# The opening of a transformer layer: token squares ahead of the transposes, modulation sums moved, first loads ahead

## The chip, the core and the metric

The kernel runs on one core of a Trainium2 chip. The metric is device time in microseconds (us). Its engines are named as in the profile: PE (TensorE, matmuls and transposes), PEld (its weight loads), DVE (VectorE), ACT (ScalarE), POOL (GpSimd) and SP (SyncE, whose queue issues nearly all loads).

## The reference

One layer of a hybrid backbone on 256 latent tokens with 256 context tokens ahead, width 2048, all in fp32. What matters here is its beginning:

```python
mod_x = jnp.split((jax.nn.silu(c) @ w_mod[l] + b_mod[l])[:, None, :], 6, axis=-1)
mod_c = jnp.split((jax.nn.silu(c_ctx) @ w_mod[l] + b_mod[l])[None, None, :], 6, axis=-1)
h   = rms_norm(x,   g_mix[l]) * (1 + mod_x[1]) + mod_x[0]
h_c = rms_norm(ctx, g_mix[l]) * (1 + mod_c[1]) + mod_c[0]
qa, ka, va, qb, kb, vb, rb, lrf, lrb, gate_a, gate_b = jnp.split(h @ w_in, offs, axis=-1)
```

The rest (windowed attention, gated linear attention, merge, output projection, ConvFFN) is the same in both kernels.

## The kernel before

**The tiling.** The 2048 input channels are 16 row blocks (kt) of 128. Every product with a weight is done in pieces: a weight tile `raw` of two row blocks by 512 columns (512 KB) is loaded, `wsplit` makes from it a rounded high part `whi` on ACT and the rest `wlo` on DVE (L61, L62), and PE adds three products (high by high, high by low, low by high) into a bank `acc` (L74). `proj_T` and `proj_nat` do this with the weight or the token side held in PE.

**The opening.** `x` and `ctx` come as four tiles of 128 tokens (1 MB each). Of each, the sum of squares is taken (the first half on ACT, L431, the second on DVE, L429), 16 transposes turn it (`ptx`, L436), and ACT and DVE copy the result to `xr` in turns. From the sums `token_rows` makes the row `rrow` of the factors 1/rms: a diagonal `dg` on DVE, two products `pr` on PE (L406), a copy on ACT.

**The modulation.** Shift and scale are SiLU(c) by columns of `w_mod`. The work is cut in five groups of row blocks, `groups = [(0, 2), (2, 2), (4, 4), (8, 4), (12, 4)]`. For each group and for shift and scale apart, `mod_both` makes a list of steps. A step loads a chunk `mraw` (1 MB) and adds its products into a bank `pm` (L302). The last step of a list also folds the sum: DVE transposes it to `mtr` (L305), PE adds the parts (`pcol`, L307), DVE makes four copies and adds the bias (L310, L313). Groups 0 and 1 have two steps in a list (chunks 256 columns wide), groups 2 to 4 have four (512 columns wide), so four steps a group and then eight.

**A group.** `affine_group` multiplies each row block of `xr` by scale and row factor on DVE (`xr`, L457), adds the shift on ACT, which gives the high part (`h00hi` for latent, `h10hi` for context, L458), and makes the low part on DVE (L459). Then the group's two row blocks (or four) go through the columns of QB (latent alone, two halves `j`), KB and VB (latent and context) of `w_in`. In group 0 ACT copies the sums out (`qb`, `kb`, `vb`, L474), later DVE adds to them (L476).

**What sets the order.** The code is written in the order of the work, and a scheduler places the instructions engine by engine; each engine then runs its list in order. `in_order` ties two instructions together without a wait. The steps of the next group's sums stand in `bg_steps`; `tick`, called ahead of each weight tile, takes from them at the rate `bg_rate`, so group 1's sums are spread over group 0's products, group 2's over group 1's, and so on. What is left is done ahead of the next group. Loads of the opening are chained in the order in which the code asks for them (`load`), on one queue. Each waits for the eighth load before it and for a free buffer: seven of `raw`, and sixteen 1 MB buffers (`M`) for all of `x`, `ctx`, `xr`, the `h` parts, `kb`, `vb`, the square's waste `junk` and the chunks `mraw`.

Of the kernel before, what the change touches and what calls it, by code (L numbers as in the profile page):

```python
# [8 lines left out]
F32 = mybir.dt.float32  # L9
# [7 lines left out]
P = 128  # L17
# [13 lines left out]
def layer_kernel(ctx, tc, A, out):  # L31
# [18 lines left out]
    def M(name, shape, dt=F32):  # L50
        return big.tile(shape, dt, name=name, tag="M")
# [20 lines left out]
    def mm(*a, **k):  # L72

        r = PE.matmul(*a, **k)  # L74
        last[0] = r.ins
        return r
# [8 lines left out]
    def mm_b(*a, **k):  # L85
        return after(PE.matmul(*a, **k))  # L86
# [100 lines left out]
    hold, last_lo = [], [None]  # L187

    def wsplit(src):
# [48 lines left out]
    def proj_T(w, c0, kts, rhs, evac):  # L238

        n = len(rhs)  # L240
        per = 2 // n
        banks = [acc.tile([P, 512], F32, name="acc", tag="acc") for _ in range(4 // per)]
        for k0 in kts[::2]:
            tick()
            nk = min(2, kts[-1] + 1 - k0)
            hi, lo = wsplit(w[k0 * P:(k0 + nk) * P, c0:c0 + 512])
            for part in range(2):
                for f in range(4):
                    for k in range(nk):
                        kt = k0 + k  # L250
                        w_ = (lo if part else hi)[:, k, f * P:(f + 1) * P]
                        for i, r in enumerate(rhs):
                            b = (f % per) if n == 1 else i
                            o = banks[f // per][:, b * T:(b + 1) * T]
                            ahi, alo = r(kt)
                            mm(o, w_, ahi, start=(kt == kts[0] and b == 0 and part == 0),
                                      stop=(kt == kts[-1] and part == 1), skip_group_check=True)
# [5 lines left out]
    behind = []  # L263

    def proj_pair(w, c0, kts, pair, banks, evac):

# [17 lines left out]

    ALL = list(range(KT))


    def mod_both(part, t0, n, dst):

        a = []  # L290
        c0, w = part * D + t0 * P, n * P
        nk = 16 // n

        def step(k0):
            if k0 == 0:
                a.append(bank(f"pm{part}_{t0}", (P, w), side=True))
            raw = M("mraw", [P, nk, w])
            load(raw, w_mod[k0 * P:(k0 + nk) * P, c0:c0 + w].rearrange("(c p) d -> p c d", p=P))
            for k in range(nk):
                kt = k0 + k  # L300
                q = 32 * (kt % 4)
                PE.matmul(a[0][q:q + 32, :], cS[:, kt, :], raw[:, k, :], start=(kt < 4), stop=(kt >= 12))  # L302
            if k0 == KT - nk:
                tr = W2("fb", "mtr", [P, n, 4, 32])
                V.transpose(tr.rearrange("p a b c -> p (a b c)"), a[0])  # L305
                pc = bank(f"pcol{part}_{t0}", (32, n * 4, 2))
                PE.matmul(pc, sel[:, 0:32], tr.rearrange("p a b c -> p (a b) c")[:, :, 0:2], start=True, stop=True)  # L307
                pv = pc.rearrange("p (a b) c -> p b c a", b=4)
                for b4 in range(4):
                    V.tensor_copy(dst[32 * b4:32 * b4 + 32, :, t0:t0 + n], pv[:, b4, :, :])  # L310
                b0 = part * 16 + t0
                d = dst[:, :, t0:t0 + n]
                V.tensor_tensor(d, d, bmod[:, b0:b0 + n].unsqueeze(1).to_broadcast([P, 2, n]), op=ALU.add)  # L313

        return [lambda k0=k0: step(k0) for k0 in range(0, KT, nk)]

    def mod_latent(parts, put=lambda fn: defer(3, fn), begin=None):

# [81 lines left out]
    def token_rows(tag, name, cols, mms=None):  # L400

        pr = bank("pr", (P, T), side=True)
        for t in range(2):
            dg = sm.tile([P, P], F32, name="dg", tag="t128", bufs=2)
            V.tensor_scalar(dg, ident, cols[:, t:t + 1], None, op0=ALU.mult)
            i = PE.matmul(pr[:, t * P:(t + 1) * P], ones[:, 0:P], dg, start=True, stop=True).ins  # L406
            if mms is not None:
                mms.append(i)
# [6 lines left out]
    mods = [mod_both(0, t0, n, shift1) + mod_both(1, t0, n, scale1) for t0, n in groups]  # L415

    xr = [M(f"xr{i}", [P, 8, T]) for i in range(4)]
    rrow1 = []
    junk = M("junk", [P, D])

    def load_tokens(s):
        ss = sm.tile([P, 2], F32, name="ss0", tag="ss0", bufs=2)
        for t in range(2):
            x_ = x00
            if s or t:
                x_ = M(f"x{s}{t}", [P, D])
                load(x_, A["ctx" if s else "x"][0][t * P:(t + 1) * P, :])
            if t:
                V.scalar_tensor_tensor(junk, x_, 1.0, x_, op0=ALU.mult, op1=ALU.mult, accum_out=ss[:, t:t + 1])  # L429
            else:  # L430
                S.activation(junk, x_, AF.Square, accum_out=ss[:, t:t + 1])  # L431
            for g in range(4):
                pt = bank("ptx", (P, 4, P), side=True)
                for k in range(4):
                    kt = g * 4 + k
                    PE.transpose(pt[:, k, :], x_[:, kt * P:(kt + 1) * P], ident)  # L436
                dst = xr[2 * s + g // 2][:, (g % 2) * 4:(g % 2) * 4 + 4, t * P:(t + 1) * P]
                if g % 2:
                    V.tensor_copy(dst, pt)
                else:  # L440
                    S.activation(dst, pt, AF.Copy)
        rrow1.append(token_rows("fa", f"rrow{s}", rms_scale(ss, D, [P, 2])))


# [4 lines left out]
    def h_all(s):  # L449
        return lambda kt: (hh[s][kt // 8][:, kt % 8, :], hl[s][kt // 8][:, kt % 8, :])  # L450
# [20 lines left out]
    def add_to(dst, first):  # L471
        def evac(i, b):
            if first:
                S.activation(dst(i), b, AF.Copy)  # L474
            else:
                V.tensor_tensor(dst(i), dst(i), b, op=ALU.add)  # L476
        return evac

    hh, hl = [], []
    for gi, (t0, n) in enumerate(groups):  # L480
        kts = ALL[t0:t0 + n]
        if gi == 0:
            load_tokens(0)
            for f in mods[0]:
                f()
        while bg_steps:
            bg_steps.pop(0)()
        if gi + 1 < len(groups):
            bg_steps.extend(mods[gi + 1])
            ticks = 4 * ((n + 1) // 2)  # L490
            bg_rate[:] = [1.4 * len(bg_steps) / ticks + 0.01, 0.0]
        for s in range(2):
            if gi == 0:
                if s:
                    load_tokens(1)
# [11 lines left out]
        proj_T(w_in, KB, kts, [h_all(0), h_all(1)], add_to(lambda i: kbt[:, i, :], gi == 0))  # L507
        proj_nat(w_in, 0, VB, kts, h_xc, add_to(lambda i: vb0[:, i, :], gi == 0))

    chain.clear()  # L510
# [618 lines left out]
```

## Time and profile before

| what | value |
|---|---|
| median of 3 runs | 2019.94 us (2017.64 to 2020.4) |
| the profiled execution | 2015.56 us, its span 2013.8 us |
| PE, DVE, ACT busy | 98%, 71%, 48% of the span |
| loads | 413.54 MB, mean 205 GB/s |

"Busy" counts the time in which an engine has an instruction under way. In the timeline a row gives the start (us from the span's start), the length of the run of equal instructions, engine, line, operation, what is written and read, and the count; in brackets stands how long the engine sat idle ahead of the row and who ended it. The products of the sums and rows (`pm`, `pcol`, `pr`) count as two instructions each in the profile; transposes and the weight products count as one.

### The profile page before, as it was taken

The page shows a single profiled execution, that of the slowest core. Times are in us where ns is not written, and L with a number is a line of the kernel's source. Part 1 is how long each engine was busy: PE and PEld are TensorE (multiplying, and loading weights), DVE is VectorE, ACT ScalarE, POOL GpSimd, SP SyncE. Part 2 cuts the span into 40 slices and gives each one's busy share as a digit, 9 for nine tenths or more (in the row PEclk, how much of TensorE's full clock was granted, in tenths as well). Part 3 has the DMA queues.
Part 4 walks back from the last instruction along what each step waited for, and adds up shares of the span by engine and source line. Part 5 has one row for each costly group of instructions (what it writes and reads, how often), then busy time and mean ns, then how long its engine had stood idle before and what let it go on. Part 6 is the DMA issues. An engine that isn't in the chain of part 4 may idle for free.

```text
span 2013.8 us, 27449 instructions
## 1 busy us (share of the span) xinstructions
PE 1971.1 (98%) x10418; PEld 1642.8 (82%) x10418; DVE 1432.6 (71%) x2237; ACT 960.8 (48%) x1394; POOL 43.9 (2%) x62
## 2 busy tenths in 40 slices
PE   6999999999999999999999999999999999999999
PEld 4679888887887777888888878888888888888887
DVE  5656567867858888978876455898888455667754
ACT  4323464553345556444444444555555334555542
POOL 0001100111000000000000000000000000000000
PEclk9999999999999999999999999999999999999999
DMA  9976223336764456888887765588876656666663
GB/s 347 385 263 196 78 83 95 84 88 202 217 181 126 116 162 199 279 287 288 289 285 232 238 201 182 175 285 257 255 247 217 214 191 193 189 190 184 194 211 114
DMA packets 214340, 413.54 MB, mean 205 GB/s; under 512 B 12548, under 2 KB 21092, under 8 KB 213184
## 3 DMA queue, kind: packets, MB, share of 16 engines
q1 hardware_dynamic: 212320, 406.89, 63.4%
q0 software_dynamic: 1360, 4.74, 0.9%
q8 instruction: 81, 1.33, 0.3%
q14 instruction: 51, 0.42, 0.1%
q10 hardware_dynamic: 528, 0.17, 0.0%
HBM read 409.63 MB, written 2.11 MB: 204 GB/s over the span
## 4 chain that ended last, share of the span: by engine, by line
PE 60%; issue 16%; DVE 0%; POOL 0%; DMA 0%; ACT 0%; POOLq 0%
PE acc L74 47%; PE accs L74 12%; PE pto L89 0%; POOL att L764 0%; DMA glan<-in_gla_norm 0%; PE ptx L89 0%; POOL att L762 0%; PE pcl L86 0%; DVE yd L1072 0%; DVE yd L1066 0%; DVE yo L964 0%; DVE wlo L62 0%; DVE og L910 0%; DVE x L965 0%; PE pr L406 0%
## 5 line engine op out<-in xcount | busy, mean ns | idle before, releaser
L61 ACT ACTIVATE whi<-raw 128x1024 fp32r<-128x1024 f32 x568 | 601.4, 1059 | 798.1 <-PE acc L74 630.5
L62 DVE TENSOR_TENSOR wlo<-raw,whi 128x1024 fp32r<-128x1024 f32 x568 | 695.2, 1225 | 389.8 <-ACT whi L61 350.5
L343 DVE SCALAR_TENSOR_TENSOR macc<-raw,ccol,macc 128x512 f32<-128x512 f32 x240 | 180.1, 750 | 3.8
L74 PE MATMUL acc<-h,whi 128*128 128x512 f32 x704 | 176.9, 393 | 0.5 <-DVE h L459 0.5
L74 PE MATMUL accs<-h,whi 128*128 128x512 f32 x704 | 176.3, 392 | 0.0
L74 PEld LDWEIGHTS acc<-h,whi 128*128 128x128 f32 x704 | 126.5, 189 | 23.5 <-DVE h L459 0.8
L74 PEld LDWEIGHTS accs<-h,whi 128*128 128x128 f32 x704 | 126.6, 189 | 22.7
L74 PE MATMUL acc<-whi,h00hi 128*128 128x512 f32 x352 | 140.9, 400 | 2.2 <-DVE v3l L62 0.5
L74 PE MATMUL acc<-whi,h01hi 128*128 128x512 f32 x352 | 139.8, 397 | 0.0
L74 PE MATMUL acc<-whi,h00lo 128*128 128x512 f32 x352 | 138.6, 394 | 0.0
L74 PE MATMUL acc<-whi,h01lo 128*128 128x512 f32 x352 | 138.1, 392 | 0.0
L74 PE MATMUL acc<-whi,al 128*128 128x512 f32 x352 | 137.1, 389 | 0.0
L74 PE MATMUL acc<-whi,ah 128*128 128x512 f32 x352 | 137.0, 389 | 0.0
L74 PEld LDWEIGHTS acc<-h,wlo 128*128 128x128 f32 x704 | 96.2, 190 | 6.9
L74 PEld LDWEIGHTS accs<-h,wlo 128*128 128x128 f32 x704 | 96.0, 190 | 6.8
L74 PE MATMUL acc<-h,wlo 128*128 128x256 f32 x704 | 98.3, 282 | 0.0
L74 PE MATMUL accs<-h,wlo 128*128 128x256 f32 x704 | 98.2, 282 | 0.0
L74 PE MATMUL acc<-wlo,h00hi 128*128 128x512 f32 x352 | 97.2, 392 | 0.0
L74 PE MATMUL acc<-wlo,h01hi 128*128 128x512 f32 x352 | 96.9, 392 | 0.0
L74 PE MATMUL acc<-wlo,ah 128*128 128x512 f32 x352 | 94.5, 389 | 0.0
L74 PEld LDWEIGHTS acc<-whi,h00hi 128*128 128x128 f32 x352 | 66.4, 189 | 16.7 <-DVE v3l L62 1.2
L74 PEld LDWEIGHTS acc<-whi,ah 128*128 128x128 f32 x352 | 66.1, 188 | 13.7
(375 smaller groups left out, 3460.8 us busy)
## 6 DMA issues: line engine op xcount, KB each, us to landing
raw<-in_w_in SPq DMA_DIRECT2D x208, 512.0 KB, 4.5
raw<-in_w_up SPq DMA_DIRECT2D x176, 512.0 KB, 4.3
raw<-in_w_mod SPq DMA_DIRECT2D x128, 512.0 KB, 4.4
raw<-in_w_down SPq DMA_DIRECT2D x88, 512.0 KB, 3.7
mraw<-in_w_mod SPq DMA_DIRECT2D x32, 1024.0 KB, 12.7
raw<-in_w_attn_o SPq DMA_DIRECT2D x32, 512.0 KB, 4.9
raw<-in_w_gla_o SPq DMA_DIRECT2D x32, 512.0 KB, 4.7
raw<-in_w_out SPq DMA_DIRECT2D x32, 512.0 KB, 3.6
```

What stands on the lines that cost most here:

```text
L61: S.activation(hi, src, AF.Copy)
L62: return V.tensor_tensor(lo, src, hi.bitcast(F32), op=ALU.subtract).ins
L74: r = PE.matmul(*a, **k)
L343: i0 = V.scalar_tensor_tensor(a[0], raw[:, k, :], ccol[:, kt:kt + 1], a[0], op0=ALU.mult, op1=ALU.add).ins
```

## The change

Seven things are done, all in the opening:

1. `load_tokens` is cut in three: the loads, then `turn_tokens` (both squares first, with a waste tile each, then all transposes and copies), then `token_factor` (the row of factors).
2. `mod_both` gives the fold apart from the steps (`end`). `both_parts` puts the fold of the shift behind the first step of the scale.
3. Group 0 is written out: two steps, the row factors, then the other steps and folds, with transposes of `ident` into an unused bank `warm` between them (34 in all). `pe_seq` ties PE's instructions there in the written order, and `behind` ties QB's first product to the last of them.
4. The loads are asked for in another order: the weights of QB (both halves), the context's two tiles, then the weights of KB and VB stand right behind group 0's four chunks. `wsplit` takes these four from `early`.
5. Group 1's sums are no longer spread over group 0's products. They are written out behind KB of group 0 and ahead of VB, and tied to follow each other.
6. The context's transposes and its row factors are tied in the same way behind QB.
7. `token_rows` gets `after`, and the fold goes through `mm_b`; both place a product behind the last weight product when `tick` calls them.

The core of the diff:

```diff
     def wsplit(src):
-        raw = wload(src)
+        raw = early.pop(0) if early else wload(src)
...
+    def pe_seq(i):
+
+        if opening and opening[0] is not i.ins:
+            in_order(opening[0], i.ins)
+            opening[:] = [i.ins]
...
             if k0 == KT - nk:
                 tr = W2("fb", "mtr", [P, n, 4, 32])
                 V.transpose(tr.rearrange("p a b c -> p (a b c)"), a[0])
-                pc = bank(f"pcol{part}_{t0}", (32, n * 4, 2))
...
+        def end():
+            pc = bank(f"pcol{part}_{t0}", (32, n * 4, 2))
+            pe_seq(mm_b(pc, sel[:, 0:32], a[1].rearrange("p a b c -> p (a b) c")[:, :, 0:2],
+                        start=True, stop=True))
...
+        return s0 + s1[:1] + [e0] + s1[1:] + [e1]
...
+    def turn_tokens(s, tiles):
+        ss = sm.tile([P, 2], F32, name="ss0", tag="ss0", bufs=2)
+        S.activation(junk, tiles[0], AF.Square, accum_out=ss[:, 0:1])
+        V.scalar_tensor_tensor(junk2, tiles[1], 1.0, tiles[1], op0=ALU.mult, op1=ALU.mult, accum_out=ss[:, 1:2])
+        for t, x_ in enumerate(tiles):
...
+    def idle(n):
+        for _ in range(n):
+            pe_seq(PE.transpose(warm[:, 0:P], ident, ident))
...
         if gi == 0:
-            load_tokens(0)
-            for f in mods[0]:
-                f()
+            x_t = load_tokens(0)
+            ss = turn_tokens(0, x_t)
+            mods[0][0]()
+            mods[0][1]()
+            token_factor(0, ss)
+            idle(8)
+            mods[0][2]()
+            idle(6)
+            mods[0][3]()
+            mods[0][4]()
+            idle(8)
+            mods[0][5]()
+            idle(12)
+            behind[:] = opening
+            opening.clear()
+            early.extend(wload(w_in[0:256, QB + j * 512:QB + j * 512 + 512]) for j in range(2))
+            x_t = load_tokens(1)
+            early.extend(wload(w_in[0:256, c:c + 512]) for c in (KB, VB))
         while bg_steps:
             bg_steps.pop(0)()
-        if gi + 1 < len(groups):
+        if 0 < gi < len(groups) - 1:
             bg_steps.extend(mods[gi + 1])
...
         proj_T(w_in, KB, kts, [h_all(0), h_all(1)], add_to(lambda i: kbt[:, i, :], gi == 0))
+        if gi == 0:
+            opening[:] = [last[0]]
+            for f in mods[1]:
+                f()
+            opening.clear()
         proj_nat(w_in, 0, VB, kts, h_xc, add_to(lambda i: vb0[:, i, :], gi == 0))
```

Three places in the engines' lists follow. First PE, from the end of QB to the start of KB in group 0 before. `x_367` and `x_394` are the context's tiles, `pm_2_457` the scale sum of group 1 (the shift sum stands ahead, among the QB products), `h10` the context's part.

```order
L74 MATMUL acc<-h00hi,wlo 128x256 x8
L436 MATMUL ptx<-ident,x_367 128x128 x16
L436 MATMUL ptx<-ident,x_394 128x128 x16
L406 MATMUL pr<-dg,ones 128x128 x2
L302 MATMUL pm_2_457<-mraw,cS 32x256 x16
L307 MATMUL pcol_2_480<-mtr,sel 32x16
L74 MATMUL acc<-h00hi,whi 128x256
```

The same engine after the change, from the middle of VB in group 0 to the first product of group 1. `pm_2_523` and `pm_2_546` are group 1's shift and scale, `pm_4_628` is group 2's shift.

```order
L74 MATMUL acc<-whi,h10lo 128x512
L312 MATMUL pm_2_523<-mraw,cS 32x256 x8
L74 MATMUL acc<-wlo,h00hi 128x512 x4
L74 MATMUL acc<-wlo,h10hi 128x512 x4
L312 MATMUL pm_2_523<-mraw,cS 32x256 x8
L312 MATMUL pm_2_546<-mraw,cS 32x256 x8
L86 MATMUL pcol_2_557<-mtr,sel 32x16
L312 MATMUL pm_2_546<-mraw,cS 32x256 x8
L86 MATMUL pcol_2_576<-mtr,sel 32x16
L312 MATMUL pm_4_628<-mraw,cS 32x512 x12
L74 MATMUL acc<-h00hi,whi 128x256
```

All four steps of group 1 now stand at the end of group 0, and only three steps of group 2 stand between the last fold and group 1's first product.

Second, ACT before, from the splits for KB and VB to those of group 1.

```order
L61 ACTIVATE whi<-raw 128x1024 x2
L458 ACTIVATE h00hi<-xr_116,shift_110 128x256 x2
L458 ACTIVATE h10hi<-xr_118,shift_110 128x256
L474 ACTIVATE kb_451<-acc 128x512 x4
L458 ACTIVATE h10hi<-xr_118,shift_110 128x256
L474 ACTIVATE vb_452<-acc 128x512 x4
L61 ACTIVATE whi<-raw 128x1024 x4
```

And after:

```order
L504 ACTIVATE kb_461<-acc 128x512 x4
L504 ACTIVATE vb_462<-acc 128x512 x4
L488 ACTIVATE h00hi<-xr_116,shift_110 128x256 x2
L488 ACTIVATE h10hi<-xr_118,shift_110 128x256 x2
L61 ACTIVATE whi<-raw 128x1024 x4
```

Group 1's four affine rows moved from among the copies of `kb` and `vb` to behind them, straight ahead of group 1's first weight.

Third, DVE at the start of group 0, before (the fold of the scale and what follows it):

```order
L310 COPY scale_111<-pcol_0_246 32x2x2 x4
L313 TENSOR_TENSOR scale_111<-scale_111,c_108 128x2x2
L464 SCALAR_TENSOR_TENSOR scale_111<-scale_111,c_108 128x2 x2
L457 SCALAR_TENSOR_TENSOR xr_116<-xr_116,scale_111,rrow_191 128x256 x2
L459 SCALAR_TENSOR_TENSOR h00lo<-xr_116,shift_110,h00hi 128x256 x2
L62 TENSOR_TENSOR wlo<-raw,whi 128x1024
```

And after:

```order
L324 COPY scale_111<-pcol_0_270 32x2x2 x4
L62 TENSOR_TENSOR wlo<-raw,whi 128x1024
L327 TENSOR_TENSOR scale_111<-scale_111,c_108 128x2x2
L494 SCALAR_TENSOR_TENSOR scale_111<-scale_111,c_108 128x2 x2
L487 SCALAR_TENSOR_TENSOR xr_116<-xr_116,scale_111,rrow_216 128x256
L62 TENSOR_TENSOR wlo<-raw,whi 128x1024
L489 SCALAR_TENSOR_TENSOR h00lo<-xr_116,shift_110,h00hi 128x256
L487 SCALAR_TENSOR_TENSOR xr_116<-xr_116,scale_111,rrow_216 128x256
```

The low parts of the first two weights moved up, one into the fold and one between the first row block's two steps.

More of the change, by code (lines that the diff above doesn't have):

```diff
@@ L187, in layer_kernel @@
     hold, last_lo = [], [None]
+    early, behind = [], []
     def wsplit(src):
-        raw = wload(src)
+        raw = early.pop(0) if early else wload(src)
         with tc.high_priority():
@@ L255, in proj_T @@
                             ahi, alo = r(kt)
-                            mm(o, w_, ahi, start=(kt == kts[0] and b == 0 and part == 0),
-                                      stop=(kt == kts[-1] and part == 1), skip_group_check=True)
+                            m = mm(o, w_, ahi, start=(kt == kts[0] and b == 0 and part == 0),
+                                   stop=(kt == kts[-1] and part == 1), skip_group_check=True)
+                            if behind:
+                                in_order(behind.pop(), m.ins)
                             if part == 0:
@@ L301, in step @@
                 q = 32 * (kt % 4)
-                PE.matmul(a[0][q:q + 32, :], cS[:, kt, :], raw[:, k, :], start=(kt < 4), stop=(kt >= 12))
+                pe_seq(PE.matmul(a[0][q:q + 32, :], cS[:, kt, :], raw[:, k, :], start=(kt < 4), stop=(kt >= 12)))
             if k0 == KT - nk:
@@ L305, in step @@
                 V.transpose(tr.rearrange("p a b c -> p (a b c)"), a[0])
-                pc = bank(f"pcol{part}_{t0}", (32, n * 4, 2))
[L307 to L315, printed above, removed]
+                a.append(tr)
+        def end():
+            pc = bank(f"pcol{part}_{t0}", (32, n * 4, 2))
+            pe_seq(mm_b(pc, sel[:, 0:32], a[1].rearrange("p a b c -> p (a b) c")[:, :, 0:2],
+                        start=True, stop=True))
+            pv = pc.rearrange("p (a b) c -> p b c a", b=4)
+            for b4 in range(4):
+                V.tensor_copy(dst[32 * b4:32 * b4 + 32, :, t0:t0 + n], pv[:, b4, :, :])
+            b0 = part * 16 + t0
+            d = dst[:, :, t0:t0 + n]
+            V.tensor_tensor(d, d, bmod[:, b0:b0 + n].unsqueeze(1).to_broadcast([P, 2, n]), op=ALU.add)
+        return [lambda k0=k0: step(k0) for k0 in range(0, KT, nk)], end
     def mod_latent(parts, put=lambda fn: defer(3, fn), begin=None):
@@ L405, in token_rows @@
             V.tensor_scalar(dg, ident, cols[:, t:t + 1], None, op0=ALU.mult)
-            i = PE.matmul(pr[:, t * P:(t + 1) * P], ones[:, 0:P], dg, start=True, stop=True).ins
+            i = after(PE.matmul(pr[:, t * P:(t + 1) * P], ones[:, 0:P], dg, start=True, stop=True))
+            pe_seq(i)
             if mms is not None:
-                mms.append(i)
+                mms.append(i.ins)
         r = W2(tag, name, [P, T])
@@ L414, in layer_kernel, with both_parts @@
     groups = [(0, 2), (2, 2), (4, 4), (8, 4), (12, 4)]
-    mods = [mod_both(0, t0, n, shift1) + mod_both(1, t0, n, scale1) for t0, n in groups]
+    def both_parts(t0, n):
+        (s0, e0), (s1, e1) = (mod_both(part, t0, n, dst) for part, dst in ((0, shift1), (1, scale1)))
+        return s0 + s1[:1] + [e0] + s1[1:] + [e1]
+    mods = [both_parts(t0, n) for t0, n in groups]
     xr = [M(f"xr{i}", [P, 8, T]) for i in range(4)]
     rrow1 = []
-    junk = M("junk", [P, D])
+    junk, junk2 = M("junk", [P, D]), M("junk2", [P, D])
     def load_tokens(s):
-        ss = sm.tile([P, 2], F32, name="ss0", tag="ss0", bufs=2)
+        tiles = []
         for t in range(2):
@@ L435, in load_tokens @@
                     kt = g * 4 + k
-                    PE.transpose(pt[:, k, :], x_[:, kt * P:(kt + 1) * P], ident)
+                    i = PE.transpose(pt[:, k, :], x_[:, kt * P:(kt + 1) * P], ident)
+                    if s == 0 and t == 0 and kt == 0:
+                        opening[:] = [i.ins]
+                    pe_seq(i)
                 dst = xr[2 * s + g // 2][:, (g % 2) * 4:(g % 2) * 4 + 4, t * P:(t + 1) * P]
@@ L479, in layer_kernel @@
     hh, hl = [], []
+    warm = acc.tile([P, 512], F32, name="warm", tag="acc")
+    def idle(n):
+        for _ in range(n):
+            pe_seq(PE.transpose(warm[:, 0:P], ident, ident))
     for gi, (t0, n) in enumerate(groups):
@@ L507, in layer_kernel @@
         proj_T(w_in, KB, kts, [h_all(0), h_all(1)], add_to(lambda i: kbt[:, i, :], gi == 0))
+        if gi == 0:
+            opening[:] = [last[0]]
+            for f in mods[1]:
+                f()
+            opening.clear()
         proj_nat(w_in, 0, VB, kts, h_xc, add_to(lambda i: vb0[:, i, :], gi == 0))
```

12 lines of the change are left out of this document (6 added, 6 removed).

## The prediction

> **What bounds the kernel now.** I read the page first, then the table of stretches, then the timelines of TensorE, VectorE and ScalarE up to 76 us, then the waits of the DMA queue.
>
> ```profile
> span 2013.8 us, 27449 instructions
> PE 1971.1 (98%) x10418; PEld 1642.8 (82%) x10418; DVE 1432.6 (71%) x2237; ACT 960.8 (48%) x1394; POOL 43.9 (2%) x62
> ```
> ```profile
> 0.00:28.20 28.20, 13.40 (x122) 8.71 (x122) 11.54 (x38) 9.69 (x15) 0.89 (x5) 0.94 0.99 320
> 28.20:61.60 33.40, 27.61 (x224) 22.09 (x224) 18.29 (x44) 17.54 (x31) 2.10 (x4) 1.00 1.05 382
> 61.60:142.00 80.40, 77.32 (x566) 58.27 (x562) 51.72 (x101) 22.28 (x31) 0.00 (x0) 1.00 0.85 309
> ```
> TensorE is busy for 98% of the span. The stretches (us from:to, length, busy PE, PEld, DVE, ACT, POOL, granted clock, DMA share, GB/s) show what is left: 14.8 us before the first product at 28.2, 5.8 us up to the start of group 1 at 61.6, 3.1 us from there to 142. In the first two the DMA engines are full (share 0.99 and 1.05): weights and waits for small vector work share the blame.
>
> TensorE's timeline, the rows that begin a piece of the opening:
>
> ```profile
> 7.95 3.87 PE L436 MATMUL ptx<-ident,x 128*128 128x128 f32 x16
> ...
> 12.60 1.53 PE L436 MATMUL ptx<-ident,x 128*128 128x128 f32 x12 [0.18 <-DVE xr L439]
> ...
> 17.96 3.06 PE L302 MATMUL pm<-mraw,cS 128*32 128x256 f32 x32
> ...
> 24.34 0.24 PE L307 MATMUL pcol<-mtr,sel 128*32 128x16 f32 x2 [0.58 <-DVE mtr L305]
> 25.61 1.07 PE L302 MATMUL pm<-mraw,cS 128*32 128x256 f32 x16 [1.03 <-DMA mraw<-in_w_mod]
> 28.21 0.39 PE L74 MATMUL acc<-h00hi,whi 128*128 128x256 f32 x1 [1.53 <-ACT whi L61]
> ...
> 36.05 1.47 PE L436 MATMUL ptx<-ident,x 128*128 128x128 f32 x12
> ...
> 43.88 0.68 PE L406 MATMUL pr<-dg,ones 128*128 128x128 f32 x4 [3.04 <-DVE dg L405]
> 44.49 1.93 PE L302 MATMUL pm<-mraw,cS 128*32 128x256 f32 x32
> 47.37 0.24 PE L307 MATMUL pcol<-mtr,sel 128*32 128x16 f32 x2 [0.95 <-DVE mtr L305]
> 47.54 0.38 PE L74 MATMUL acc<-h00hi,whi 128*128 128x256 f32 x1
> ...
> 54.09 0.50 PE L74 MATMUL acc<-whi,h00hi 128*128 128x512 f32 x1 [0.54 <-ACT kb L474]
> ...
> 59.75 1.92 PE L302 MATMUL pm<-mraw,cS 128*32 128x512 f32 x16
> 61.61 0.39 PE L74 MATMUL acc<-h00hi,whi 128*128 128x256 f32 x1
> ...
> 71.54 2.78 PE L302 MATMUL pm<-mraw,cS 128*32 128x512 f32 x24
> ```
> Group 0 has products from 28.21 (QB), 47.54 (KB) and 54.09 (VB). The sums for group 1 stand at 25.61, in the QB products, and at 44.49; 47.37 is the last fold. They are finished 14 us before group 1 needs them at 61.61: all that group 1 does with them on DVE and ACT lies under KB and VB. That is the cover which the change takes away.
>
> **The change part by part.** All modulation data come by one queue, and the start doesn't move: two token halves and four chunks are still the first six loads. The pm at 25.61 waited for the fifth chunk; a chunk is 1.05 MB, at 350 GB/s (320 with the start-up) 3.0 us, so the fourth landed at about 22.5, and the fold at 24.34 stays. Both squares first, the row factors behind two steps, shift fold one step later: all this lies ahead of the fourth chunk and is worth nothing. The 34 warm transposes at 0.13 each (12 in 1.53) are 4.3 us of PE work inside the 14.8 us that wait; only eight stand close before a fold (about 0.1 lost).
>
> From there VectorE and ScalarE decide:
>
> ```profile
> 24.62 0.65 DVE L310 COPY scale<-pcol 32x4 f32<-32x4 f32 x4 [0.33 <-PE pcol L307]
> 25.30 0.16 DVE L313 TENSOR_TENSOR scale<-scale,c 128x4 f32<-128x4 f32 x1
> 25.50 0.23 DVE L464 SCALAR_TENSOR_TENSOR scale<-scale,c 128x2 f32<-128x2 f32 x2
> 25.78 0.88 DVE L457 SCALAR_TENSOR_TENSOR xr<-xr,scale,rrow 128x256 f32<-128x256 f32 x2
> 26.84 0.88 DVE L459 SCALAR_TENSOR_TENSOR h00lo<-xr,shift,h00hi 128x256 fp32r<-128x256 f32 x2 [0.18 <-ACT h00hi L458]
> 28.19 1.23 DVE L62 TENSOR_TENSOR wlo<-raw,whi 128x1024 fp32r<-128x1024 f32 x1 [0.46 <-ACT whi L61]
> ```
> ```profile
> 27.11 1.04 ACT L61 ACTIVATE whi<-raw 128x1024 fp32r<-128x1024 f32 x1
> ...
> 34.22 1.92 ACT L431 ACTIVATE junk<-x 128x2048 f32<-128x2048 f32 x1 [1.28 <-DMA x<-in_ctx]
> ...
> 60.43 1.08 ACT L61 ACTIVATE whi<-raw 128x1024 fp32r<-128x1024 f32 x1
> ```
> *First product.* Now whi is early (first weights land right behind the fourth chunk), but two wlo of 1.23 stand in DVE's order inside the chain: copies to 25.27, wlo to 26.4, add and scale to 26.7, xr 27.1, h00hi (0.5) 27.6. First product about 27.7, 0.5 earlier. The second row block passes another wlo, then the context square of 1.92 ahead of its h00hi on ACT: 30.2. QB is 48 products at 0.12 (28.21 to 36.05 holds 48, 16 pm like those of 1.07, and a fold); 40 are left at 30.2, so QB ends at 35.0: 1.0 earlier than 36.05.
>
> *Context.* Its data lie there, and the VectorE square is done ahead; the 3.04 us wait at 43.88 shrinks to about the rest of the chain of small steps. Transposes 35.0 to 39.8 with eight KB products between, pr at 41.0, context half of KB at 43.3 (0.4 row, 0.5 xr, 0.5 h10hi and their hand-overs; I take 2.3). Then 40 KB products (4.8), 24 VB products at 0.23 (54.09 to 59.75; 5.5) and all four steps of group 1 (twice 1.93): the last pm ends at 57.5, the last fold comes 0.95 later, 58.5. Before, PE had all this at 59.75: **1.2 us gained up to here.**
>
> *Group 1's start.* Behind that fold stands a chain with no products over it: 24.34 to 25.78, 1.44 from fold to first xr; on DVE six of the seven xr and lo (0.40 each) ahead of the last xr, 2.4, and it 0.48; on ACT h10hi 0.5, and only then whi 1.06, since ACT's order has all four affine rows first. 58.5 + 1.44 + 2.4 + 0.48 + 0.5 + 1.06 = 64.4, say 64.3 as the last two overlap. PE fills 2.8 of it with three pm steps of group 2 (2.78 for 24), one more than before (0.93), and waits 2.7. So group 1 starts 2.7 later with 0.93 more done: **1.75 us behind.** The gain of 1.2 has become a loss.
>
> *The queue.* The third chunk of group 2 now needs the slot of group 1's first chunk, which PE frees only in VB, near 53.
>
> ```profile
> SPq L95 <- PE pm L302: 45.9, 10, 22.0
> ```
> ```profile
> 111.63 2.53 SPq L95 DMA_DIRECT2D raw<-in_w_in  x1
> 136.22 4.43 SPq L95 DMA_DIRECT2D mraw<-in_w_mod  x2
> ```
> ```profile
> mraw<-in_w_mod SPq DMA_DIRECT2D x1, 1024.0 KB, 5.1
> ```
> The queue waits in order, as it did for 22 us after 111.63; a chunk issued into the then empty engines took 5.1 us (the one at 136.22). Ahead of that chunk stand 16.8 MB: 9.0 by 28.2 and the rest at 382 GB/s, landed by 48.6 to 50. So the DMA engines run dry for some 5 us, and the chunk lands at 58.1. PE wants it third, at 60.4: no wait. Five chunks and two weights behind it (6.3 MB, 16.5 us) land by 74.6; before, PE took the last one at 73.4 (71.54 plus two steps), now 75.1. It just fits; and a PE that came to group 1 without any wait would find that chunk 1.2 later than it took it before. Chain and queue set the same loss, one by itself.
>
> Behind group 1's first product all engines keep their order but for a few folds. Waits that depend on DVE (0.54 at 54.09 and its like) shrink when PE is late; I take 0.25 for that. **Sum: +1.5 us.** Bounds: the group-1 chain between 2.2 (ACT and DVE fully overlapped) and 3.2 of wait gives +1.0 to +2.0; the recovery 0 to 0.6.
>
> The profiled execution took 2015.56 (1.8 around its span), so 2017.1 after; the median of the runs is 4.4 higher, and the forecast is made against it: 2019.94 + 1.5 = **2021.4 us**.
>
> **The rivals.** (A) *The clock, ending slower.*
>
> ```profile
> 15.21:18.62 3.41, 1.27 (x16) 0.94 (x20) 2.05 (x9) 0.79 (x3) 0.00 (x0) 1.00 1.09 348
> 18.63:22.00 3.37, 2.82 (x30) 1.18 (x26) 0.55 (x2) 0.00 (x0) 0.00 (x0) 0.50 1.09 348
> ...
> 39.10:42.50 3.40, 1.53 (x12) 1.29 (x12) 3.40 (x6) 1.39 (x4) 0.00 (x0) 1.00 1.07 365
> ```
> After 1.27 us of work in 3.4 the granted clock fell to 0.50 for 3.4 us; after 1.53 it didn't. The change's PE has about 1.1 us of work between 25.8 and 30.2: a stretch of 3.4 us inside it would halve the clock under the QB products, 1.0 to 1.7 us, and a start of group 1 shifted so may halve it again, 1.7. It decides from two such stretches: 1.5 + 1.0 + 1.7 = 4.2, 2024.2. For it: the gap is longer than those at 39. Against: warm transposes fill up to 25.8, and where a stretch begins is open. Chance 0.2 for one or two (2022.5 to 2024.5).
>
> The Trainium skill, "TensorE: Matmul & The Clock Gate", Part 4, says that transposes don't count as busy for that gate. By that rule the warm ones hold nothing. The trace speaks against it: transposes alone ran 16 in 3.87, then 12 in 1.53, so they did raise the clock. In a rival of its own, transposes don't hold it: then 1.0 us of pm is all the work from 22.5 to 27.7, and both that stretch's successors run at half, another 1.0 us by the QB products: 2022.5 to 2025, chance 0.05.
>
> (B) *The queue decides.* The margin at 75.1 is 0.5. A dry spell of 7 instead of 5 puts PE's wait at 1.5 to 2: 2023. For it: PE's first pm may be later than 53; against: the pm stands ahead of VB's second half. Chance 0.08.
>
> (C) *Faster.* If group 1's affine work hid (say whi taken ahead of it), PE would have its 1.2 and the 0.9 in hand, 2.1; that lasts only if the hole in the queue is smaller too, since the chunk at 74.6 takes it back. With PE's first pm of group 1 at 50 instead of 53 both hold: -2 us, 2018. Against: ACT's order is fixed, and KB's context half can't start before pr. Chance 0.09. A gain over 0.2% has no mechanism here; I leave 0.08 for one that I do not see.
>
> (D) *The change does nothing*: the scheduler moved shift folds back beside their sums in group 2; within 0.5 of 2019.9. It is inside the forecast's range.
>
> **The numbers.** A measurement of this kernel can tell about 0.2%, 4 us, from no change. Forecast (2020.4 to 2022.5, the likeliest) 0.50 with D; A 0.2 and, for the rule on transposes, 0.05; B 0.08; C 0.09; unseen 0.08. Runs of the kernel before spread over 2.8 us, so the range is 2017.0 to 2024.8. Slower than 2024.0: half of A, half of the rival on transposes, some of B and of the unseen, 0.18. Faster than 2015.9: 0.08. The rest, 0.74, is within.
>
> **What would show it.** Right: first product near 27.7, context half of KB near 43, last pm of group 1 near 57.5, then PE idle for 2 to 3 us on ACT's whi, group 1 near 64.3, and a hole of some 5 us in the DMA row around 50. Wrong: group 1 starting before 62, no hole, or clock 0.50 anywhere behind 22 us. If from 142 on the stretches differ in PE time, my sum looked at the wrong place.

## The result, and the profile after

| | median | runs |
|---|---|---|
| before | 2019.04 us | 20 (2015.38 to 2021.06) |
| changed | 2021.89 us | 20 (2018.63 to 2025.74) |

The ratio is 1.0014 (95% interval 1.0008 to 1.0020): 2.85 us slower, inside the 0.2% bound and inside the range; the forecast was 2021.4. The granted clock is the share of its full speed at which TensorE was let run. The profiled execution of the changed kernel is one of its long ones (2024.45 us, mean granted clock 0.995). At its two ends the 20 runs go with their clock: the four at 0.999 took 2018.63 to 2020.61, the three at 0.995 took 2023.87 to 2025.74; those between overlap with both. So the trace is read for two things that have to be held apart, the order of the work and the clock. Of the experiments below, one execution lies far from the rest, one of e1's twelve (6988.5 us); without it e1's median is 2014.89 instead of 2015.06 us.

The stretches of the changed kernel (columns as before: us from:to, length, busy PE, PEld, DVE, ACT, POOL, granted clock, DMA share, GB/s). The first two answer to the stretches shown of before; the others are places where the clock or the queue gave way:

```profile
28.20:61.60 33.40, 29.29 (x204) 25.52 (x205) 12.69 (x24) 14.66 (x27) 2.09 (x4) 0.85 0.77 261
61.60:142.00 80.40, 74.64 (x537) 56.13 (x534) 53.86 (x115) 22.49 (x33) 0.00 (x0) 0.96 0.97 357
...
52.00:58.00 6.00, 6.00 (x44) 4.50 (x43) 0.00 (x0) 1.89 (x4) 0.00 (x0) 1.00 0.00 0
```
```profile
27.26:30.67 3.41, 1.47 (x8) 1.06 (x8) 2.56 (x6) 2.48 (x3) 0.00 (x0) 1.00 0.99 396
44.33:47.74 3.41, 1.77 (x12) 1.61 (x13) 1.92 (x5) 1.29 (x3) 2.09 (x4) 1.00 1.05 382
64.81:68.22 3.41, 1.32 (x14) 0.16 (x4) 2.83 (x8) 1.97 (x5) 0.00 (x0) 1.00 1.05 388
```
```profile
30.67:37.50 6.83, 5.84 (x27) 5.85 (x28) 2.89 (x5) 2.53 (x6) 0.00 (x0) 0.50 1.07 356
47.74:51.15 3.41, 3.41 (x18) 3.41 (x17) 0.00 (x0) 0.00 (x0) 0.00 (x0) 0.50 0.68 243
68.22:75.04 6.82, 5.98 (x28) 5.40 (x32) 2.73 (x4) 0.79 (x1) 0.00 (x0) 0.50 1.05 387
```
The hole in the queue is there: 6 us without a byte, where the prediction had some 5. Three times a stretch of 3.41 us with 1.3 to 1.8 us of PE work was followed by half clock, for 6.8, 3.4 and 6.8 us: 17 us at half, where the profiled execution of before had 3.4.

TensorE's timeline, the rows that answer to those of before:

```profile
10.51 0.28 PE L124 MATMUL pc<-ident,crow 32*128 32x32 f32 x1 [10.51 <-DMA ident<-in_k_ident]
...
28.49 0.73 PE L74 MATMUL acc<-h00hi,whi 128*128 128x256 f32 x4 [1.87 <-ACT h00hi L488]
...
31.66 1.22 PE L74 MATMUL acc<-h00hi,whi 128*128 128x256 f32 x4 [1.44 <-ACT h00hi L488]
...
46.65 0.74 PE L74 MATMUL acc<-h10hi,whi 128*128 128x256 f32 x4 [1.53 <-ACT h10hi L488]
...
63.31 0.20 PE L86 MATMUL pcol<-mtr,sel 128*32 128x16 f32 x1 [0.59 <-DVE mtr L315]
...
69.06 0.58 PE L74 MATMUL acc<-h00hi,whi 128*128 128x256 f32 x1 [2.93 <-ACT whi L61]
```
And what DVE and ACT do between the last fold and group 1's first product:

```profile
63.58 0.65 DVE L324 COPY scale<-pcol 32x4 f32<-32x4 f32 x4 [0.33 <-PE pcol L86]
...
64.66 1.28 DVE L487 SCALAR_TENSOR_TENSOR xr<-xr,scale,rrow 128x256 f32<-128x256 f32 x3
65.86 0.87 DVE L489 SCALAR_TENSOR_TENSOR h00lo<-xr,shift,h00hi 128x256 fp32r<-128x256 f32 x2
66.65 0.48 DVE L489 SCALAR_TENSOR_TENSOR h10lo<-xr,shift,h10hi 128x256 fp32r<-128x256 f32 x1
67.05 0.48 DVE L487 SCALAR_TENSOR_TENSOR xr<-xr,scale,rrow 128x256 f32<-128x256 f32 x1
```
```profile
67.56 0.51 ACT L488 ACTIVATE h10hi<-xr,shift 128x256 fp32r<-128x256 f32 x1 [1.07 <-DVE xr L487]
67.97 1.04 ACT L61 ACTIVATE whi<-raw 128x1024 fp32r<-128x1024 f32 x1
```
The chain from the fold to whi stands in the written order, with PE idle 2.93 us at its end. From 142 us on the distance to before stays: matched product by product, the changed kernel's profiled execution is 8.89 us behind at the 350th weight product and 8.88 at the 8600th. All of the difference between these two executions arises in the opening.

### The profile page after: what moved, and what is told of

Same layout as the page of the kernel before. It is cut to its first block, busy times and chain, and to the rows that moved or that the text cites. A ratio compares the mean times of both kernels' runs of the same rounds, so it can differ in the third digit from the quotient of the medians.

```text
span 2022.7 us, 27506 instructions
## 1 busy us (share of the span) xinstructions
PE 1979.6 (98%) x10452; PEld 1652.0 (82%) x10452; DVE 1432.4 (71%) x2237; ACT 961.6 (48%) x1394; POOL 43.2 (2%) x62
## 4 chain that ended last, share of the span: by engine, by line
PE 59%; issue 16%; DVE 0%; POOL 0%; DMA 0%; ACT 0%; POOLq 0%
PE acc L74 46%; PE accs L74 12%; PE pto L89 0%; POOL att L822 0%; DMA glan<-in_gla_norm 0%; PE ptx L89 0%; POOL att L820 0%; PE pcl L86 0%; DVE yd L1130 0%; DVE yd L1124 0%; DVE yo L1022 0%; DVE wlo L62 0%; DVE og L968 0%; DVE x L1023 0%; PE pr L420 0%
## 5 line engine op out<-in xcount | busy, mean ns | idle before, releaser
L74 PEld LDWEIGHTS acc<-whi,ah 128*128 128x128 f32 x352 | 66.1, 188 | 13.6
```

## The experiments

Times compare with before in the same session, whose median was 2020.13 (e1 to e4), 2020.36 (e5 to e8) and 2020.56 us (e9 to e11). Two theories were held against each other: **S**, the place of group 1's sums (the chain without cover, the late slot), and **K**, the clock.

**e4: the clock held.** Transposes are put into the waits. For those between the row blocks the edit also sorts the products of QB's first piece by row block.

```diff
-            idle(12)
+            idle(20)     # behind group 0's last fold
+            idle(10)     # between QB's first two row blocks
+            fill(12)     # behind the context's row factor
+            fill(18)     # ahead of group 1's first product
```


> The changed kernel with more warm transposes in the waits where the clock fell: 8 more behind the last fold, 10 between the two row blocks of the first QB piece, 12 behind the context's row factor, 18 ahead of group 1's first product. Theory K: granted clock 1.00 from 14 us on in nearly all executions, and the time is that of the changed kernel's executions with mean clock 0.999 (2018.6 to 2020.6, mean 2019.6). Theory S: the clock is held, but the wait on whi and the hole stay, so it lies 0.5 to 1.5 above the kernel before and no lower: about 2020. If transposes do not hold the clock: 2021.9 or more.

Measured: 2019.95 us, 0.9999 of before (0.9991 to 1.0008), against 1.0014 for the changed kernel: 1.9 us less by the medians, 3.0 by the two ratios; mean clock 0.9994 over its runs (0.9972 for the changed kernel). The four runs at 1.000 took 2016.23 to 2017.98; the other seven (0.999) took 2019.95 to 2024.56, so e4's median is not one of a clock held throughout. TensorE's timeline of e4, at full clock throughout:

```profile
43.33 0.73 PE L74 MATMUL acc<-h10hi,whi 128*128 128x256 f32 x4 [0.22 <-ACT h10hi L499]
...
58.51 0.20 PE L86 MATMUL pcol<-mtr,sel 128*32 128x16 f32 x1 [0.59 <-DVE mtr L326]
...
61.27 2.18 PE L530 MATMUL fill<-ident 128*128 128x128 f32 x18
64.27 0.38 PE L74 MATMUL acc<-h00hi,whi 128*128 128x256 f32 x1 [0.82 <-ACT whi L61]
...
75.83 1.07 PE L323 MATMUL pm<-mraw,cS 128*32 128x512 f32 x8 [0.57 <-DMA mraw<-in_w_mod]
```
This is the trace that the prediction described: the context half of KB at 43.33 (predicted 43.3), the last fold at 58.51 (58.5), group 1's first product at 64.27 (64.3), behind 3.0 us of filled and idle wait on whi (2.7). Both theories hold a part: K these 1.9 to 3.0 us, S what stays.

**e10: the same for the kernel before.**

```diff
+        idle(20, ...)      # ahead of each row factor
         rrow1.append(token_rows(...))
+            idle(6, warm)  # behind group 0's last fold
+            idle(10, warm) # ahead of the first product
```


> The kernel before with warm transposes in its waits (20 ahead of each row factor, 6 behind the last fold of group 0, 10 ahead of the first product) and nothing else. If most of the 4.4 us between the profiled execution of before (2015.56, mean clock 0.999) and the median of its runs (2019.9, 0.994 to 0.997) is the clock: 2015 to 2017 with mean clock 0.999, and the change then costs 2 to 5 us at equal clock (e4_more_warm 2019.95). If it is not: 2019 to 2020.

Measured: 2017.11 us, 0.9987 of before (0.9978 to 0.9995), mean clock 0.9993. The stretch of 13.7 us ahead of the first product, in e10 and then in before (granted clock third from the right):

```profile
14.50:28.20 13.70, 10.31 (x124) 6.93 (x124) 7.10 (x29) 2.35 (x6) 0.00 (x0) 1.00 1.09 352
```
```profile
14.50:28.20 13.70, 7.16 (x88) 3.46 (x88) 7.21 (x30) 2.64 (x6) 0.00 (x0) 0.88 1.09 352
```
Only transposes were added, and up to 145 us the orders of PE, DVE and ACT differ from before in three small shifts (one fold a few products later, two neighbours swapped twice on ACT). So 3.45 us of before's own median goes with the clock. Of 80 runs of before in these sessions 79 have a mean clock of 0.994 to 0.997 and one 0.998; the execution that was profiled had 0.999 and is among the fastest. With the transposes in both, the change costs 2.4 us by the ratios of e4 and e10 to before (0.9999 less 0.9987) and 2.84 by their medians. Among the executions at 1.000 alone, four of each, it costs 1.0 by the means (2017.32 against 2016.30). In the two traces e4 is 1.6 us behind e10 at the 350th weight product, when the opening is over, and 0.4 at the last; where the rest is given back in small pieces I did not follow up.

**e7: sums early, clock held; and e11: one fold back.** In e7 two of group 1's steps stand ahead of the context's row factor, the rest and both folds behind it (the scheduler puts them among KB's products), with e4's transposes up to QB and eight behind the row factor. In e11 the last fold alone goes behind VB.

```diff
                     ss = turn_tokens(1, x_t)
+                    mods[1][0]()
+                    mods[1][1]()
                     token_factor(1, ss)
+                    fill(8)
+                    for f in mods[1][2:]:    # e11: [2:5]
+                        f()
...
         proj_nat(w_in, 0, VB, ...)
+        mods[1][5]()                         # e11 only
```


> e1_sums_among_context with warm transposes in the waits at 26, 30 and 42 us. Theory K: the one fall of the clock left in e1 (45.7 to 49.1) goes, worth up to 1.7: about 2013.3, mean clock 0.999 or 1.0 in nearly all executions, and less spread than e1 (2013.8 to 2018.3). If warm transposes stand in the way of the products they cost as much as they give: 2014.9.

> e7_sums_early_warm with one thing moved: the last fold of group 1 (one product of 0.2 us, with its five small VectorE steps) stands behind VB; all four steps of sums, and so the slots and the loads, stay early. If the chain behind the fold is the loss: fold near 59.7, first product of group 1 5.9 later (1.44 + 2.4 + 0.48 + 0.5 + 1.06) near 65.5 instead of 62.4, TensorE idle some 3 us on whi, no hole; 2.5 to 3.5 above e7, up to 5 where the clock falls in that wait: 2017.5 to 2019.5. If the place of the sums' products or the late slots are the loss: as e7, 2014.9.

Measured: e7 2014.93 us (0.9974 of before, 0.9965 to 0.9983), e11 2016.86 (0.9986, 0.9977 to 0.9995). One product of 0.2 us in another place costs 1.9 us, less than the 2.5 that I had put as the least. The start of group 1 in e7, TensorE and ScalarE:

```profile
59.63 2.78 PE L319 MATMUL pm<-mraw,cS 128*32 128x512 f32 x24
62.34 0.38 PE L74 MATMUL acc<-h00hi,whi 128*128 128x256 f32 x1
```
```profile
60.30 1.08 ACT L61 ACTIVATE whi<-raw 128x1024 fp32r<-128x1024 f32 x1
```
And in e11:

```profile
58.58 0.20 PE L86 MATMUL pcol<-mtr,sel 128*32 128x16 f32 x1
...
64.33 0.39 PE L74 MATMUL acc<-h00hi,whi 128*128 128x256 f32 x1 [2.93 <-ACT whi L61]
```
```profile
63.24 1.04 ACT L61 ACTIVATE whi<-raw 128x1024 fp32r<-128x1024 f32 x1
```
In e7 whi is ready while PE still adds group 2's sums. In e11 all of the affine work stands behind the fold: 5.75 us from fold to first product (5.9 expected), of which group 2's sums fill 2.74, and PE is idle for the same 2.93 us as in the changed kernel. Product by product, e11 goes from 1.05 us ahead of e7 (in VB) to 1.98 behind (in group 1) and stays there, all at full clock: 3.0 us at the place, 1.9 in the medians. The chain is shown, and its price.

**e5: the slots free early, the chain left.** e4 with the first two steps behind the row factor, the folds at the end.

```diff
                     token_factor(1, ss)
+                    fill(8)
+                    mods[1][0]()
+                    mods[1][1]()
...
-            for f in mods[1]:
+            for f in mods[1][2:]:
```


> The kernel e4_more_warm (clock held) with the first two of group 1's four steps moved into the context's wait, behind the row factor: the slots of their chunks come free some 9 us earlier; both folds stay at the end of group 0, so the chain behind them is as it was. If the late slot (the hole in the queue) is the loss: no hole, no wait of TensorE on mraw in group 2, and 2 or more below e4_more_warm (fast executions 2016.2 to 2018.0). If the chain is: TensorE still waits on whi at group 1's first product (18 warm transposes and about 0.8 idle in e4), and only the two steps' 1.9 us of PE work is saved, less what it costs in KB: 0.5 to 2 below e4.

Measured: 2020.13 us, e4's time (both 0.9999 of before). Four microseconds of the hole, in e5 and then in e4:

```profile
50.00:54.00 4.00, 4.00 (x24) 3.50 (x23) 0.00 (x0) 1.88 (x4) 0.00 (x0) 1.00 1.05 388
```
```profile
50.00:54.00 4.00, 4.00 (x30) 2.65 (x29) 0.00 (x0) 0.21 (x1) 0.00 (x0) 1.00 0.11 39
```
The DMA engines are full again, and the 0.57 us wait on mraw that e4 has at 75.83 is gone; the time is not. The 1.9 us of the two steps went into KB's products instead of a wait (VB begins 2.8 us later than in e4), so my "0.5 to 2 below" missed, and the chain still ends at 65.27. So closing the hole gains nothing while the chain sets the start; whether it would cost anything without the chain no run shows.

**e1 and e2: the sums' place with everything else as it was.** e1 is the changed kernel with the sums as in e7 and no added transposes; e2 is the kernel before with only the sums moved late.

```diff
-        if gi + 1 < len(groups):
+        if 0 < gi < len(groups) - 1:
...
         proj_T(w_in, KB, ...)
+        mods[1].pop(0)()           # e2: first step
         proj_nat(w_in, 0, VB, ...)
+        while mods[1]:             # e2: the others
+            mods[1].pop(0)()
```


> The changed kernel with one thing moved: the sums and folds of group 1 stand among the context's small steps and the KB products instead of behind KB; nothing is left out. Theory S (the place of the sums: a chain without cover at the start of group 1, and the slot of the first chunk freed late): no wait of TensorE on whi at group 1's first product (2.93 us now), no hole in the DMA row between 52 and 58, 1.5 to 3 us less than the changed kernel: 2019 to 2020.4. Theory K (the clock alone: it fell to half three times in the profiled execution): only the third fall, at 68, goes, those at 30 and 47 stay: 2021 or more.

> The kernel before with only the sums of group 1 moved to the end of group 0 (first step behind KB, the others behind VB). Theory S: PE idle 2 to 3 us on whi at group 1's start and a DMA hole, 1.5 to 3 us slower than before: 2020.5 to 2022. Theory K: the same as before within 0.7 us, since the gap at 25 to 30 us is the old one; a fall of the clock at group 1's start alone would add at most 1.7.

Measured: e1 2015.06 us (0.9978 of before, 0.9969 to 0.9987), 6.8 less than the changed kernel, under what I expected. Its profiled execution has one fall of the clock (45.71 to 49.12) instead of three, so part of the 6.8 may be the clock. But holding it as well gains nothing here: e7, which is e1 with transposes in the waits, has a mean clock of 0.9995 instead of 0.9985 and took 2014.93, where theory K expected 2013.3, and in the traces the two are within 0.2 us of each other at the 350th weight product. e2 2029.86 (1.0044, 1.0032 to 1.0056), 9.7 above before, far more than I expected. TensorE in e2 at group 1's start:

```profile
67.89 0.20 PE L86 MATMUL pcol<-mtr,sel 128*32 128x16 f32 x1 [0.59 <-DVE mtr L305]
...
73.64 0.39 PE L74 MATMUL acc<-h00hi,whi 128*128 128x256 f32 x1 [3.79 <-ACT whi L61]
```
The fold-to-product chain is again 5.75 us. The rest of the 9.7 I can only bound: two of the four steps (1.93) lay in before's wait for the context and now lie on the path, and the mean clock is 0.9952, against 0.996. So late sums cost 7 us on the one kernel and 10 on the other, the clock included, and the other six edits, with the sums early but not in before's place, give about 5 (e1 against before).

**e3 and e8: no warm transposes** in the changed kernel and in e1.

```diff
-        for _ in range(n):
+        for _ in range(0):
             pe_seq(PE.transpose(warm[:, 0:P], ident, ident))
```


> The changed kernel without its 34 warm transposes. If transposes hold the clock: it falls between 18 and 25 us, so that sums, folds and first QB products run at half; 1 to 3 us slower than the changed kernel (2023 to 2025), unless all of it lies under the loads. If they do not count for the clock (the rule of the Trainium skill's page TensorE: Matmul & The Clock Gate, Part 4): the clock has the same falls as in the changed kernel, and the time is the same, 2021.9.

> e1_sums_among_context without any warm transpose. If the warm ones only shift the first fall of the clock (as the pair changed kernel and e3_no_warm says, 2021.89 and 2021.93): 2014.9 as e1, with lower mean clock. If they hold it where no later wait takes it away again: 1.5 to 3.5 slower, 2016.5 to 2018.5.

Measured: e3 2021.93 us (changed kernel 2021.89; by the ratios to before, 1.0009 and 1.0014, 1 us less), e8 2014.91 (e1 2015.06). The 34 transposes gain no time. They do change the clock: means 0.9963 without, 0.9972 with them, and 0.9974 and 0.9985 for the other pair. e3's stretches around the first fall:

```profile
23.12:26.53 3.41, 1.09 (x18) 0.40 (x10) 2.30 (x11) 2.01 (x2) 0.00 (x0) 1.00 1.06 413
26.53:33.35 6.82, 5.12 (x22) 4.83 (x23) 5.01 (x7) 3.02 (x5) 0.00 (x0) 0.50 1.02 391
```
The fall comes at 26.53 instead of 30.67 and lasts as long: the transposes end at 26.6, 1.87 us ahead of the first product, and seem only to shift it. That is one trace of each, and the stretches begin at different times in them. Where more transposes shorten that wait (e4, e10), the clock holds.

**e6: the vector engines' order as well.** e7 with the two wlo tied behind the first two row blocks on DVE and the context's square behind them on ACT (16 transposes ahead of the first product, none between the row blocks).

```diff
+        in_order(affine_last[0], square)     # ACT
+        hold.extend([affine_last[1]] * 2)    # DVE, both wlo
```


> The sums among the context's work (e1), warm transposes in the waits, and the first affine rows ahead of the two wlo on VectorE and of the context's square on ScalarE. If the vector order held the first products back: first product at 27.3 and second row block by 28.6 (28.5 and 31.0 in e1), 1.5 to 2.5 less than e7_sums_early_warm: about 2011. If the start of KB's context half is set by something else (context data and row factor), the gain at QB is gone by 44 us and the time equals that of e7.

Measured: 2012.78 us, 0.9966 of before (0.9953 to 0.9978), the fastest here: 2.2 under e7, 9.1 under the changed kernel, 7.6 under before. TensorE from the fold to the first product in e6, then in e7:

```profile
28.34 0.23 PE L86 MATMUL pcol<-mtr,sel 128*32 128x16 f32 x2
...
30.86 0.74 PE L74 MATMUL acc<-h00hi,whi 128*128 128x256 f32 x4 [0.39 <-ACT h00hi L497]
```
```profile
25.97 0.23 PE L86 MATMUL pcol<-mtr,sel 128*32 128x16 f32 x2
...
29.54 0.62 PE L74 MATMUL acc<-h00hi,whi 128*128 128x256 f32 x3 [1.00 <-ACT h00hi L495]
...
31.34 1.25 PE L521 MATMUL warm<-ident 128*128 128x128 f32 x10
```
Fold to product is 2.5 us instead of 3.6, and the second row block follows without a gap. The clock rose late in this execution of e6 (22.16), so its fold is 2.4 us behind e7's; by VB the two are level. So the traces do not show that the early products make the 2.2 us between the medians; where these come from is open.

**e9: the clock raised ahead of the tokens.**

```diff
+    for _ in range(24):
+        wi = PE.matmul(pw, ones, ones, start=True, stop=True)
```


> e6_best_order with 24 idle products of a constant tile ahead of the first transposes, so that the clock rises before the tokens come (in e6's profiled execution it rose only at 22.16). If the late rise costs time: first product at 27.3 and QB done by 34, 0.5 to 2 below e6 (2012.78), with less spread. If the start of KB's context half and the loads set it anyway: the same, 2012.8.

Measured: 2015.44 us, mean clock 0.997, 2.7 us above e6's median; the intervals against before overlap (0.9967 to 0.9986, and 0.9953 to 0.9978 for e6). Two stretches of e9:

```profile
5.47:12.30 6.83, 4.54 (x39) 4.10 (x37) 1.28 (x4) 4.82 (x6) 0.00 (x0) 1.00 1.00 286
12.30:22.54 10.24, 8.31 (x49) 6.11 (x53) 5.34 (x14) 2.63 (x7) 0.00 (x0) 0.50 1.09 351
```
The clock was up at 5.47, but the idle products end at 8.77 and PE then waits 2.0 us for `ident`; it falls at 12.30 and stays down for 10 us.

## Why the prediction came out right

**The sum.** Predicted +1.5, within +1.0 to +2.0, by the order of the work. With transposes in both it is 1.6 at the end of the opening in the traces of e4 and e10, 1.0 among their executions at 1.000, 2.4 to 2.8 in all their runs, and +2.85 for the kernels as they are. So the direction and the mechanism were right, but +2.85 is above the sum's own bounds, and it is luck that the forecast of 2021.4 is only 0.5 off: it stood on a median of three runs, 2019.94, and that of twenty is 2019.04.

One of the prediction's own signs of being wrong did come: the clock was at 0.50 behind 22 us. In the changed kernel's profiled execution the context half of KB starts at 46.65 and group 1 at 69.06, not 43 and 64.3; only e4, with the clock held, has the times that were named.

**The chain** (a wait of 2.7, a term of 1.75): right. The wait is 2.93 in the changed kernel and 3.0 in e4 (18 transposes and 0.82 idle), whose three rows named above fit to 0.1 us; e11 gives the price of the chain alone, 1.9 in the runs and 3.0 at the place.

**First product** (27.7; second row block 30.2): too early by 0.8 and 1.5; it came at 28.49 and 31.66. The step that failed is "the fold at 24.34 stays", and with it "copies to 25.27": the fold stood at 24.93, its copies ended at 25.85, and the first wlo, xr and h00hi followed with the lengths that I had put. The eight transposes close before the fold, put at 0.1, are some 0.4 of this: in e3, which lacks them, the fold stands at 24.55 and the first product at 28.06.

```profile
24.93 0.23 PE L86 MATMUL pcol<-mtr,sel 128*32 128x16 f32 x2
```
```profile
25.20 0.65 DVE L324 COPY scale<-pcol 32x4 f32<-32x4 f32 x4 [0.69 <-PE pcol L86]
```
```profile
27.93 0.51 ACT L488 ACTIVATE h00hi<-xr,shift 128x256 fp32r<-128x256 f32 x1 [0.17 <-DVE xr L487]
29.20 1.91 ACT L453 ACTIVATE junk<-x 128x2048 f32<-128x2048 f32 x1 [0.76 <-DMA x<-in_ctx]
...
31.11 0.49 ACT L488 ACTIVATE h00hi<-xr,shift 128x256 fp32r<-128x256 f32 x1
```
For the second row block the wait ahead of the context's square was left out: ACT waits for the square's data until 29.20, and h00hi, which stands behind it, starts at 31.11. Up to KB it cost nothing: in e4, with the same 28.48, the context half starts at 43.33, where the row factor allows it.

**The start "doesn't move"**: it did. `ident` landed at 10.5 and the transposes began at 10.7 instead of 7.95. As the sums wait for the fourth chunk, this cost nothing that I could see.

**The queue.** Right in place and size (6 us dry, in e4 0.11 of DMA time at 50 to 54), and right that it was not the bound: in e4 PE waits 0.57 us for the chunk that "just fits". "Chain and queue set the same loss, one by itself" is shown for one half only: the chain alone (e11) sets its loss, and e5 closes the hole without a gain while the chain stays.

**Rival A, the clock**: it happened in the profiled execution, by the mechanism named, in the two places named and once more in KB. A chance of 0.2 was too low: 16 of the 20 runs have a mean clock of 0.998 or less. Its threshold was wrong: after 1.53 us of work in 3.4 the clock had stayed up in before, after 1.77 it fell here. And it was no rival but a state of both kernels: I took the profiled execution of before as typical, whose clock had fallen once, and put its 4.4 us below the median down to nothing. By e10, 3.45 us of that median goes with the clock. What the clock costs is 3.0 us for the changed kernel (e4) and 2.6 for before (e10) by the ratios, 1.9 and 3.45 by the medians. The sum counted with neither; that the two largely cancel is luck as well.

**The rival on transposes**: refuted for the transposes of this kernel. By the Trainium skill, "TensorE: Matmul & The Clock Gate", Part 4, transposes don't count as busy for the gate. These, recorded as MATMUL with `ident`, do: e10 differs from before by transposes alone but for the three small shifts, and its mean clock is 0.9993 instead of 0.9960; e4, which also sorts a piece of QB, has 0.9994 instead of the changed kernel's 0.9972. Whether these use the transpose mode of which the page speaks, the trace does not show.

**B** (the queue decides) and **D** (nothing changes) are out by e5 and by the traces. **C** (faster) was wrongly priced: with group 1's work hidden the kernel is 5 (e7 against e4) to 7 us (e1) faster than the changed one, not 3.4, but there the steps of the sums moved too; the chain alone is 1.9 (e11).

## What to carry to other kernels

Before moving a step to a later place, follow its last small instruction to the next large one on the path: here one fold of 0.2 us has 5.75 us of dependent work behind it, and the lost cover cost more (1.9 us in e11 against e7) than the 1.2 us that the prediction had gained up to there. A profiled execution is one draw: compare its mean clock with that of the other runs before its time is used as the base of a sum. Ask where idle matmul work ends: here, where it left 1.87 or 2.0 us of waiting (changed kernel, e9), the clock still fell, and where it left 1.0 us or less (e4, e6) it held. And ask what the clock is worth in that place: from e8 over e1 to e7 the mean clock rose from 0.9974 to 0.9995, and the time stayed within 0.2 us.

## What the runs showed of the hardware

- The clock is granted in stretches of 3.41 us, or multiples, whose beginning differs from execution to execution (first change at 11.8, 13.6, 15.0 and 16.2 us in four traces). The same gap in the program may or may not halve it, which is part of the spread of the runs. In all thirteen traces, from the first rise to the program's end, every such stretch at full clock with 1.47 us of PE work or less was followed by half clock; from 1.50 to 1.88 us it went either way (1.50 held in e3 at 64.07 and 1.72 in before at 25.45; 1.77 fell here and 1.88 in e1 at 42.30). e5's profiled execution lost one such stretch far from the opening; the stretches ahead of the fall and in it:

```profile
1202.50:1205.93 3.43, 1.36 (x7) 0.79 (x5) 2.48 (x4) 1.09 (x2) 0.00 (x0) 1.00 0.61 234
1205.93:1209.34 3.41, 3.37 (x10) 2.90 (x11) 2.37 (x3) 1.91 (x5) 0.00 (x0) 0.50 0.45 154
```
- Between e4 and e7 the medians differ by 5.0 us, the traces (both at full clock) by 2.7, and the executions at 1.000 by 3.0 (means 2017.32 of four and 2014.36 of seven). The other 2 us go with e4's seven executions at 0.999. Those lie 3.9 above its other four, more than the 1.7 us that one stretch of 3.4 us at half clock can take by itself; where the rest comes from is open.
